# Weight parts of the expert layer made three pieces ahead, with ACT and DVE in program order

## The chip, the core and the metric

The kernel runs on one core of one Trainium2 chip. The core has a matrix engine (TensorE, called PE in the profile, with its weight loads as PEld), a vector engine (DVE), a scalar engine (ACT), a general-purpose engine (POOL), a queue engine (SP) that here only starts DMAs, and 16 DMA engines. The metric is the device time of one execution in microseconds (us); lower is better.

## The reference, cut to what matters

A trunk of two layers over 256 tokens of width 1024. Each layer has a mixer (attention and a delta rule) with a normalization, then a channel mixer with another. The channel mixer of the first layer is dense; that of the second sends each token to 2 of 8 experts. The change is in this expert layer alone:

```python
def swiglu(x, w_gate, w_up, w_down):
    return (jax.nn.silu(x @ w_gate) * (x @ w_up)) @ w_down
...
    gates = jax.nn.softmax(top_val, axis=-1)
...
        xb = xf[tok_b]
        return swiglu(xb, w_gate[e_b], w_up[e_b], w_down[e_b])
```

An expert has a gate and an up matrix of 1024 x 3584 and a down matrix of 3584 x 1024, all float32. Each expert's rows are weighted by its gate value and added to the tokens that chose it.

## The kernel before

**Pieces.** All expert weights stream once from HBM. A piece is what one DMA brings: 128 rows of 1792 columns of gate or up (896 KB), or two rows per partition of down (1 MB). `load` (line 148) takes one of eight raw buffers (seven in `ring`, one in `ring2`) and starts the DMA on SP; loads keep their program order. `halves` (line 163) makes of each half of a piece a high part `wh`, a rounded copy by ACT (line 178), and a low part `wl`, the difference by DVE (line 181). These take eight slots (four in `wpool`, four in `wpool2`), so four pieces can stand made. A float32 product is then three matmuls, high by high, high by low and low by high.

**Order of the work.** `experts` (line 981) runs over eight jobs, expert 0 first and the others in the order `TURN`. Three experts with few tokens are narrow (64 rows); the five others are wide (128 rows). Narrow and wide ones alternate: the third job follows the second as wide after narrow, and so on to the last two, both wide. The hidden width comes in two chunks of 1792. A chunk runs eight gate pieces, then three down pieces of the chunk before (the pending chunk), then eight up pieces and the four remaining down pieces. A wide piece is 12 matmuls (six per half). A narrow one is eight, since high and low tokens stand side by side; its eighth gate and up piece is not split but multiplied as float32 from the raw buffer, after `leads` (line 1115) has copied half of the four banks into `room`, and four matmuls with `shift` add those halves back.

**Side steps.** After the gate, ACT writes Silu into `hh` (line 1193); after the up, DVE multiplies it (line 1216). `to_features` (line 1126) then transposes `hh` on PE, and ACT and DVE split it into `hT`. `combine` (line 1089) splits the result `ys` of the expert before, multiplies it with a 0/1 matrix `DT` and adds it into `x_tok` on DVE (line 1100); `transposed` (line 1034) makes `DT`, DVE then PE then DVE. `dispatch` (line 1004) gathers the tokens of coming experts. These run as `side` steps, one after each gate or up piece.

**Who sets the order.** The framework's scheduler orders each engine's queue by its own estimate of when operands are ready, the program order as priority. `pin` (line 97) keeps an instruction in program order among the pinned ones of its engine. Before the change the DMAs, Silu, the `room` copies, the multiplication with Silu and a few steps of `dispatch` are pinned; the making of the parts, `hT`, `ys`, `DT` and the additions into `x_tok` are not, nor are the matmuls. The code that makes parts stands just ahead of its products:

```python
                for sub in in_pieces(wg, c, len(first or ()), narrow):
                    if narrow and sub[0] == KD - 1:
                        subs = next(downs, None)
                        moves = leads(banks)
                    products(banks, xg, narrow, *sub, x32)
                    if side and sub[0]:
                        side.pop(0)()
```

## Time and profile before

| what | value |
|---|---|
| median of 3 runs | 1490.4 us (1489.93 to 1492.49) |
| the profiled execution | 1489.22 us |
| its span, first to last instruction | 1487.1 us |
| mean granted clock of TensorE, of full speed | 0.989 |
| expert weights read by DMA | 128 gate and 128 up loads of 896 KB, 110 down loads of 1 MB and five smaller ones |

The profiled execution lies 1.2 us below the median of the runs, and 2.1 us lie outside its span. Line numbers are those of the kernel before. An engine's busy time is the union of its instructions; a wait is idle time of an engine, put down to what ended it. The buffers `ps_mm` and `ps_gd` hold gate and up sums, `ps_b` the down sums, `ps_a` transposes and other short uses.

### The profile page before, as it was taken

The numbers are of one execution on the slowest core, as the hardware profiler recorded it, in microseconds if no ns is written. First come the engines' busy times: TensorE is split into PE (matmuls) and PEld (weight loads), VectorE is DVE, ScalarE is ACT, GpSimd is POOL, SyncE is SP. The second block draws the span as 40 slices with busy tenths as digits, with TensorE's granted clock in tenths as the row PEclk, the third lists the DMA queues.
The fourth block names the chain that finished last, engine by engine and source line by source line (L and its number), as shares of the span: only waits on it lengthen the run. The fifth ranks groups of instructions, "written<-read, shape, count | busy, mean of one in ns | idle before, by whom it ended". The sixth has DMA issues, their size and how long they took to land.

```text
span 1487.1 us, 24022 instructions
## 1 busy us (share of the span) xinstructions
PE 1444.9 (97%) x8864; PEld 1230.1 (83%) x8864; DVE 1218.2 (82%) x1609; ACT 1037.7 (70%) x1553; POOL 23.8 (2%) x37
## 2 busy tenths in 40 slices
PE   8999999999999999999999999999999999999995
PEld 8978899998978898876698877688877589888884
DVE  6886655556797898989899989899989899989886
ACT  5747444456667577786797886886887878778763
POOL 1100000000000000000000000000000000000000
PEclk9999999999999999999999999999999999999998
DMA  9633455545533199999999999999999999999890
GB/s 323 220 115 121 161 194 179 196 125 189 199 108 129 50 337 346 376 359 353 416 404 375 381 359 391 377 409 404 355 370 401 349 404 415 344 350 392 291 374 33
DMA packets 89125, 433.93 MB, mean 292 GB/s; under 512 B 7817, under 2 KB 9993, under 8 KB 74913
## 3 DMA queue, kind: packets, MB, share of 16 engines
q1 hardware_dynamic: 87808, 428.54, 76.8%
q0 software_dynamic: 1184, 3.71, 0.9%
q8 instruction: 73, 1.20, 0.3%
q14 instruction: 60, 0.48, 0.1%
HBM read 431.17 MB, written 1.05 MB: 291 GB/s over the span
## 4 chain that ended last, share of the span: by engine, by line
PE 87%; DVE 7%; issue 2%; ACT 2%; DMA 0%; DVEq 0%; SPq 0%; ACTq 0%
PE ps_b L101 26%; PE ps_mm L101 25%; PE ps_gd L101 24%; PE ps_a L101 9%; DVE wl L181 4%; PE ps_a L1138 2%; ACT wh L178 1%; DVE x_in L1100 1%; PE ps_mm L567 0%; ACT junk L416 0%; DVE hT L1141 0%; ACT xT L241 0%; PE ps_gd L409 0%; PE ps_mm L671 0%; DVE o L1280 0%
## 5 line engine op out<-in xcount | busy, mean ns | idle before, releaser
L181 DVE TENSOR_TENSOR wl<-raw,wh 128x896 fp32r<-128x896 f32 (+2 forms) x851 | 927.5, 1143 | 146.7 <-ACT wh L178 139.6
L178 ACT ACTIVATE wh<-raw 128x896 fp32r<-128x896 f32 (+2 forms) x851 | 793.0, 996 | 147.4 <-PE ps_gd L101 70.9
L101 PE MATMUL ps_b<-wh,hT 128*128 128x512 f32 x816 | 232.5, 396 | 0.7 <-ACT hT L1140 0.7
L101 PE MATMUL ps_gd<-wh,xg 128*128 128x448 f32 x808 | 218.6, 368 | 0.0
L101 PE MATMUL ps_mm<-wh,xg 128*128 128x448 f32 x808 | 212.4, 372 | 0.3
L101 PEld LDWEIGHTS ps_b<-wh,hT 128*128 128x128 f32 x816 | 151.9, 188 | 39.4 <-issue 6.4
L101 PEld LDWEIGHTS ps_gd<-wh,xg 128*128 128x128 f32 x808 | 151.8, 188 | 12.9
L101 PEld LDWEIGHTS ps_mm<-wh,xg 128*128 128x128 f32 x808 | 147.6, 189 | 16.5 <-ACT wh L178 2.0
L101 PE MATMUL ps_b<-wl,hT 128*128 128x512 f32 x492 | 159.0, 399 | 2.3 <-DVE wl L181 2.2
L101 PE MATMUL ps_gd<-wl,xg 128*128 128x448 f32 x488 | 143.1, 374 | 8.9 <-DVE wl L181 7.2
L101 PE MATMUL ps_mm<-wl,xg 128*128 128x448 f32 x488 | 140.8, 369 | 0.1
L101 PEld LDWEIGHTS ps_b<-wl,hT 128*128 128x128 f32 x492 | 90.8, 188 | 32.0 <-DVE wl L181 6.7
L101 PEld LDWEIGHTS ps_gd<-wl,xg 128*128 128x128 f32 x488 | 89.0, 188 | 27.9 <-DVE wl L181 20.0
L101 PEld LDWEIGHTS ps_mm<-wl,xg 128*128 128x128 f32 x488 | 90.8, 188 | 11.7 <-DVE wl L181 4.3
L1140 ACT ACTIVATE hT<-ps_a 128x512 fp32r<-128x512 f32 (+2 forms) x52 | 27.4, 544 | 65.8 <-PE ps_a L1138 38.7
L101 PE MATMUL ps_mm<-xT,wh 128*128 128x256 f32 x448 | 70.9, 280 | 0.0
L101 PEld LDWEIGHTS ps_mm<-xT,wh 128*128 128x128 f32 x448 | 60.8, 189 | 0.4
L1141 DVE TENSOR_TENSOR hT<-ps_a,hT 128x512 fp32r<-128x512 f32 (+2 forms) x52 | 31.9, 621 | 26.7 <-ACT hT L1140 26.7
L101 PE MATMUL ps_gd<-xT,wh 128*128 128x256 f32 x320 | 50.5, 280 | 0.0
L1093 ACT ACTIVATE ys<-ps_b 128x512 fp32r<-128x512 f32 x14 | 8.4, 599 | 55.5 <-PE ps_b L101 41.3
L101 PE MATMUL ps_mm<-xT,wl 128*128 128x256 f32 x224 | 44.7, 280 | 0.0
L101 PEld LDWEIGHTS ps_gd<-xT,wh 128*128 128x128 f32 x320 | 43.1, 189 | 0.0
(407 smaller groups left out, 1654.3 us busy)
## 6 DMA issues: line engine op xcount, KB each, us to landing
raw<-in_moe_w_gate_dram SPq DMA_DIRECT2D x128, 896.0 KB, 8.7
raw<-in_moe_w_up_dram SPq DMA_DIRECT2D x128, 896.0 KB, 6.4
raw<-in_moe_w_down_dram SPq DMA_DIRECT2D x110, 1024.0 KB, 8.1
raw<-in_w_in_dram SPq DMA_DIRECT2D x24, 1024.0 KB, 6.9
raw<-in_ffn_w_gate_dram SPq DMA_DIRECT2D x11, 1024.0 KB, 5.1
raw<-in_ffn_w_up_dram SPq DMA_DIRECT2D x11, 1024.0 KB, 5.1
raw<-in_ffn_w_down_dram SPq DMA_DIRECT2D x11, 1024.0 KB, 4.9
raw<-in_w_out_dram SPq DMA_DIRECT2D x8, 1024.0 KB, 4.9
```

Source lines behind the costliest of these rows:

```text
L101: return PE.matmul(o, lhsT, rhs, start=start, stop=stop, skip_group_check=True)
L178: high = S.activation(wh[:, c:c + n], w, AF.Copy)
L181: low = V.tensor_tensor(wl[:, c:c + n], w, wh[:, c:c + n].bitcast(F32), op=ALU.subtract)
L1093: S.activation(yh, py[i], AF.Copy)
L1100: V.scalar_tensor_tensor(o, pt, jobs[n][2][:, b], o, op0=ALU.mult, op1=ALU.add)
L1138: PE.transpose(pt[:, f * w:(f + 1) * w], hv[:, f0 + f], ident[rows, rows])
L1140: S.activation(hT[:, f0:f0 + n_, 0], pv, AF.Copy)
L1141: V.tensor_tensor(hT[:, f0:f0 + n_, 1], pv, hT[:, f0:f0 + n_, 0].bitcast(F32), op=ALU.subtract)
```

## The change

A generator `stream` lists all pieces in the order in which the products use them. `made` loads one and makes its parts; `take` keeps a queue so that, when a piece is handed to its products, the three after it have been emitted. The instructions on ACT and DVE in the expert layer (making of parts, gathered tokens, `DT`, `ys`, `hT`, additions) are pinned. Silu now stands after one down piece and not two, the multiplication after one and not two, and the routing's `rest` runs as a side step in expert 0's first gate. The matmuls stay unpinned, and the order of the loads is the same.

```diff
@@ -38,6 +39,7 @@
...
+AHEAD = 3
...
@@ -176,9 +178,13 @@
             for c in range(0, m, n):
                 w = raw[:, i * m + c:i * m + c + n]
                 high = S.activation(wh[:, c:c + n], w, AF.Copy)
+                if extra:
+                    pin(high)
                 if fence_high[0] is not None:
                     order(high, fence_high[0])
                 low = V.tensor_tensor(wl[:, c:c + n], w, wh[:, c:c + n].bitcast(F32), op=ALU.subtract)
+                if extra:
+                    pin(low)
                 if fence[0] is not None:
                     order(low, fence[0])
             yield i * (nk // count), wh, wl
@@ -985,6 +991,7 @@
 
...
-                        S.activation(xg[:, k], i, AF.Copy)
+                        pin(S.activation(xg[:, k], i, AF.Copy))
...
-            V.tensor_tensor(x_, xg[:, KD - 1, 0].bitcast(F32), xg[:, KD - 1, 1].bitcast(F32), op=ALU.add)
+            pin(V.tensor_tensor(x_, xg[:, KD - 1, 0].bitcast(F32), xg[:, KD - 1, 1].bitcast(F32), op=ALU.add))
...
         def transposed(n):
             Dt = mp.tile([P, NB, P], F32R, tag="ys", name=nm("D"))
-            slots(Dt, jobs[n], True)
+            pin(slots(Dt, jobs[n], True))
             DT = mp.tile([P, NB, P], F32R, tag=f"DT{n % 2}", name=nm("DT"), bufs=1)
             pt = bank("a")
             for b in range(NB):
                 PE.transpose(pt[:, b * P:(b + 1) * P], Dt[:, b].bitcast(F32), ident)
-            V.tensor_copy(DT.rearrange("p b t -> p (b t)"), pt[:, 0:NB * P])
+            pin(V.tensor_copy(DT.rearrange("p b t -> p (b t)"), pt[:, 0:NB * P]))
             return DT
-        def in_pieces(w, c, k0=0, narrow=False):
...
-        def down_pieces(n, c, first=0, parts=1, cut=1):
...
+        def stream():
+            behind = []
+            for n in range(NE):
+                for c in range(NC):
+                    yield from ((n, 0, c, k) for k in range(KD))
+                    yield from behind[:3]
+                    yield from ((n, 1, c, k) for k in range(KD))
+                    yield from behind[3:]
+                    behind = [(n, 2, c, f) for f in range(0, NF, 2)]
+            yield from behind
+        def made(n, i, c, k):
+            cs = slice(c * CHUNK, (c + 1) * CHUNK)
+            if i == 2:
+                src = weights(n, 2)[cs].rearrange("(p j) d -> p j d", j=NF)[:, k:k + 2, :]
+                end = (n, c) == (NE - 1, NC - 1)
+                cut = 2 if end and k == NF - 2 else 1
+                return [(k + j, wh, wl) for j, wh, wl in piece(src, 2, D, 2 if end and k >= NF - TAIL else 1, cut)]
+            if first and (n, i, c) == (0, 0, 0) and k < len(first):
+                return list(first[k])
+            src = weights(n, i).rearrange("(k p) c -> p k c", p=P)[:, k:k + 1, cs]
+            if jobs[n][3] and k == KD - 1:
+                return load(src, 1, CHUNK)[0]
+            return list(piece(src, 1, CHUNK))
+        specs = stream()
+        ready = collections.deque()
+        ahead = AHEAD if extra else 1
+        def take():
+            for spec in itertools.islice(specs, ahead + 1 - len(ready)):
+                ready.append(made(*spec))
+            return ready.popleft()
...
-                S.activation(yh, py[i], AF.Copy)
-                V.tensor_tensor(yl, py[i], yh.bitcast(F32), op=ALU.subtract)
+                pin(S.activation(yh, py[i], AF.Copy))
+                pin(V.tensor_tensor(yl, py[i], yh.bitcast(F32), op=ALU.subtract))
...
-                    V.scalar_tensor_tensor(o, pt, jobs[n][2][:, b], o, op0=ALU.mult, op1=ALU.add)
+                    pin(V.scalar_tensor_tensor(o, pt, jobs[n][2][:, b], o, op0=ALU.mult, op1=ALU.add))
...
-                S.activation(hT[:, f0:f0 + n_, 0], pv, AF.Copy)
-                V.tensor_tensor(hT[:, f0:f0 + n_, 1], pv, hT[:, f0:f0 + n_, 0].bitcast(F32), op=ALU.subtract)
+                pin(S.activation(hT[:, f0:f0 + n_, 0], pv, AF.Copy))
+                pin(V.tensor_tensor(hT[:, f0:f0 + n_, 1], pv, hT[:, f0:f0 + n_, 0].bitcast(F32), op=ALU.subtract))
...
-        most = rest() if rest else None
+        most = []
+        if rest:
+            side = [lambda: None] * 2 + [lambda: most.append(rest())]
         for n, job in enumerate(jobs):
             narrow = job[3]
             rows = slice(0, 64) if narrow else slice(0, P)
             xg = xgs.pop(n)
             x32 = as_one(xg) if narrow else None
-            wg, wu = (weights(n, i).rearrange("(k p) c -> p k c", p=P) for i in range(2))
             for c in range(NC):
+                def project(banks, start):
+                    moves = ()
+                    for k in range(KD):
+                        parts = take()
+                        if narrow and k == KD - 1:
+                            moves = leads(banks)
+                        products(banks, xg, narrow, k, parts, x32)
+                        if side and k >= start:
+                            side.pop(0)()
+                    while side:
+                        side.pop(0)()
+                    return moves
+                def more(times=1):
+                    for _ in range(times if pend else 0):
+                        down(take(), *pend)
                 banks = gu_banks()
-                for k, f in enumerate(first or ()):
-                    products(banks, xg, narrow, k, f)
-                downs = down_pieces(pend[0], pend[1]) if pend else iter(())
-                subs, moves = None, ()
-                for sub in in_pieces(wg, c, len(first or ()), narrow):
-                    if narrow and sub[0] == KD - 1:
-                        subs = next(downs, None)
-                        moves = leads(banks)
-                    products(banks, xg, narrow, *sub, x32)
-                    if side and sub[0]:
-                        side.pop(0)()
-                first = None
+                moves = project(banks, 1)
                 fence[0] = fence_high[0] = None
-                while side:
-                    side.pop(0)()
                 hh = mp.tile([P, CHUNK], F32, tag="hh", name=nm("hh"))
                 if pend and not pend[3]:
                     pend[3].extend([bank("b"), bank("b")])
-
-                def more(subs=None):
-                    subs = subs or next(downs, None)
-                    if subs:
-                        down(subs, *pend)
-
-                more(subs)
+                more()
                 for move in moves:
                     move()
-                more()
                 for i, p in enumerate(banks):
                     pin(S.activation(hh[rows, i * BANK:(i + 1) * BANK], p[rows, :], AF.Silu))
-                more()
+                more(2)
                 banks = gu_banks()
                 if c == NC - 1 and groups and n + 1 not in xgs:
                     group = groups.pop(0)
                     tiles, side = dispatch([jobs[g] for g in group])
                     xgs.update(zip(group, tiles))
-                subs, moves = None, ()
-                for sub in in_pieces(wu, c, 0, narrow):
-                    if narrow and sub[0] == KD - 1:
-                        subs = next(downs, None)
-                        moves = leads(banks)
-                    products(banks, xg, narrow, *sub, x32)
-                    if side:
-                        side.pop(0)()
-                while side:
-                    side.pop(0)()
-                more(subs)
+                moves = project(banks, 0)
+                more()
                 for move in moves:
                     move()
-                more()
                 for i, p in enumerate(banks):
                     h = hh[rows, i * BANK:(i + 1) * BANK]
                     pin(V.tensor_tensor(h, h, p[rows, :], op=ALU.mult))
-                for subs in downs:
-                    down(subs, *pend)
+                more(3)
                 hT, side = to_features(hh, narrow)
                 if pend and pend[1] == NC - 1:
                     side += combine(pend[0], pend[3], DT)
@@ -1230,10 +1252,8 @@
         while side:
             side.pop(0)()
         f0 = c * NF
-        TAIL = 4
-        for subs in itertools.islice(down_pieces(n, c), (NF - TAIL) // 2):
-            down(subs, *pend)
-        subs = [(f0 + f, wh, wl) for subs in down_pieces(n, c, NF - TAIL, 2, 2) for f, wh, wl in subs]
+        more((NF - TAIL) // 2)
+        subs = [(f0 + f, wh, wl) for _ in range(TAIL // 2) for f, wh, wl in take()]
         extra.clear()
 
         par = ring.tile([P, 2, D], F32, tag="raw", name=nm("par"))
...
-        return most
+        return most[0] if most else None
```

## Rows read from the trace of the kernel before

**Rows 1.** the page: its span, and busy time, share and instructions of each engine

```profile
span 1487.1 us, 24022 instructions
PE 1444.9 (97%) x8864; PEld 1230.1 (83%) x8864; DVE 1218.2 (82%) x1609; ACT 1037.7 (70%) x1553; POOL 23.8 (2%) x37
```

**Rows 2.** busy time by stretch: length, PE, PEld, DVE, ACT, POOL (instructions), clock, DMA share, GB/s

```profile
617.50:848.00 230.50, 227.03 (x1047) 184.60 (x1047) 210.51 (x225) 182.25 (x242) 0.00 (x0) 1.00 0.97 381
...
1312.20:1434.40 122.20, 121.50 (x585) 107.03 (x584) 110.21 (x118) 94.39 (x113) 0.00 (x0) 1.00 0.93 347
```

**Rows 3.** busy time by stretch, same columns: one pair of experts in five stretches

```profile
848.00:905.50 57.50, 57.24 (x253) 44.22 (x252) 51.11 (x55) 49.08 (x64) 0.00 (x0) 1.00 0.98 373
905.50:938.80 33.30, 31.27 (x135) 22.33 (x134) 28.18 (x31) 20.78 (x30) 0.00 (x0) 1.00 0.96 368
938.80:963.80 25.00, 24.14 (x95) 15.89 (x94) 23.25 (x25) 23.58 (x29) 0.00 (x0) 1.00 0.98 381
963.80:1017.10 53.30, 53.30 (x257) 46.90 (x256) 50.48 (x52) 43.71 (x53) 0.00 (x0) 1.00 1.01 412
1017.10:1079.30 62.20, 61.66 (x313) 54.73 (x312) 58.11 (x65) 46.10 (x70) 0.00 (x0) 1.00 0.97 372
```

**Rows 4.** busy time by stretch of the down sums alone: length, PE, PEld, DVE, ACT

```profile
848.00:905.50 57.50, 24.90 (x103) 18.78 (x102) 0.00 (x0) 0.00 (x0) 1.00 0.98 373
905.50:938.80 33.30, 10.40 (x43) 7.50 (x42) 1.37 (x2) 1.20 (x2) 1.00 0.96 368
938.80:963.80 25.00, 7.05 (x27) 4.62 (x26) 0.00 (x0) 0.00 (x0) 1.00 0.98 381
963.80:1017.10 53.30, 12.59 (x51) 9.10 (x50) 0.00 (x0) 0.00 (x0) 1.00 1.01 412
1017.10:1079.30 62.20, 15.65 (x65) 11.54 (x64) 1.37 (x2) 1.20 (x2) 1.00 0.97 372
```

**Rows 5.** timeline of PE: start, length of the merged run, instruction, count

```profile
585.81 1.10 PE L101 MATMUL ps_b<-wh,hT 128*128 128x512 f32 x4
...
587.21 1.09 PE L101 MATMUL ps_b<-wh,hT 128*128 128x512 f32 x4
...
594.15 0.98 PE L101 MATMUL ps_mm<-wh,xg 128*128 128x448 f32 x4
...
595.38 0.98 PE L101 MATMUL ps_gd<-wh,xg 128*128 128x448 f32 x4
...
596.61 0.59 PE L101 MATMUL ps_a<-D,xs 128*128 128x192 f32 x4
597.03 0.39 PE L101 MATMUL ps_mm<-wh,xg 128*128 128x448 f32 x1
```

**Rows 6.** busy time of raw-buffer instructions alone, same columns; PE is the unsplit part

```profile
905.50:938.80 33.30, 3.22 (x8) 1.01 (x8) 22.73 (x21) 15.25 (x18) 0.00 (x0) 1.00 0.96 368
```

**Rows 7.** waits, 905.5 to 938.8 us: total us, times, longest

```profile
ACT ys L1093 <- PE ps_b L101: 4.8, 1, 4.8
...
ACT hh L1193 <- PE ps_mm L101: 2.1, 1, 2.1
...
ACT room L1122 <- PE ps_mm L101: 2.0, 1, 2.0
```

**Rows 8.** timeline of DVE around the second narrow gate's Silu

```profile
932.98 3.50 DVE L181 TENSOR_TENSOR wl<-raw,wh 128x1024 fp32r<-128x1024 f32 x3 [0.38 <-ACT wh L178]
939.73 4.23 DVE L181 TENSOR_TENSOR wl<-raw,wh 128x1024 fp32r<-128x1024 f32 x4 [3.26 <-ACT wh L178]
```

**Rows 9.** timeline of ACT, the same stretch

```profile
931.88 2.95 ACT L178 ACTIVATE wh<-raw 128x1024 fp32r<-128x1024 f32 x3
936.92 0.97 ACT L1193 ACTIVATE hh<-ps_mm 64x448 f32<-64x448 f32 x2 [2.09 <-PE ps_mm L101]
938.64 5.26 ACT L178 ACTIVATE wh<-raw 128x1024 fp32r<-128x1024 f32 x6
```

**Rows 10.** waits, 1017.1 to 1079.3 us, with a combining step: total, times, longest

```profile
DVE x_in L1100 <- PE ps_a L101: 0.9, 2, 0.7
```

More of the change, by code (lines that the diff above doesn't have):

```diff
@@ L1 @@
+import collections
 import itertools
@@ L987, in experts @@
         NC = FE // CHUNK
+        TAIL = 4
         def xg_tile(narrow):
@@ L1040, in transposed @@
                 PE.transpose(pt[:, b * P:(b + 1) * P], Dt[:, b].bitcast(F32), ident)
-            V.tensor_copy(DT.rearrange("p b t -> p (b t)"), pt[:, 0:NB * P])
+            pin(V.tensor_copy(DT.rearrange("p b t -> p (b t)"), pt[:, 0:NB * P]))
             return DT
-        def in_pieces(w, c, k0=0, narrow=False):
-            for k in range(k0, KD):
-                src = w[:, k:k + 1, c * CHUNK:(c + 1) * CHUNK]
-                yield k, load(src, 1, CHUNK)[0] if narrow and k == KD - 1 else piece(src, 1, CHUNK)
         def products(outs, xg, narrow, k, parts, x32=None):
@@ L1066, in products @@
                         mm(o[j], x_, w[:, j * BANK:(j + 1) * BANK], k == 0 and w is wh, False)
-        def down_pieces(n, c, first=0, parts=1, cut=1):
-            wd = weights(n, 2)[c * CHUNK:(c + 1) * CHUNK].rearrange("(p j) d -> p j d", j=NF)
-            for f in range(first, NF, 2):
-                yield [(f + j, wh, wl) for j, wh, wl in piece(wd[:, f:f + 2, :], 2, D, parts, cut if f == NF - 2 else 1)]
+        def stream():
[28 more added lines that the diff above has]
+            return ready.popleft()
         def down(subs, n, c, hT, py):
```

## The prediction

> **What bounds the kernel now.** I read the page first, then busy time by stretch, then the down sums alone, then the timelines and waits where an engine pauses. On the page PE is busy for 97% of the span, its weight loads for 83% and DVE for 82% [rows 1]; so PE looks full. The stretches say more. The steady part of the expert layer repeats: a narrow and a wide expert take 230.5 and 231.3 us in the first two of three pairs, and the last wide expert 122.2 us [rows 2, 3]. I cut one pair into the narrow expert's first chunk, its second gate, its second up, and the wide expert's two chunks [rows 3].
>
> Next, what PE needs in each. In undisturbed work six matmuls of 512 columns start 1.40 us after one another (585.81 to 587.21), six of 448 columns 1.23 us; that is 0.233 and 0.205 us each. Four gathering matmuls of 192 columns take 0.42 us, 0.105 each; transposes are taken at the same, an estimate [rows 5]. The unsplit narrow part takes 3.2 us a phase [rows 6], its four shift matmuls 0.8 at 0.205. The code gives the gate and up matmuls (56 a narrow phase, 96 a wide one), the trace the down ones: 103, 43, 27, 51 and 65 [rows 4]; a combining step adds eight of 512 columns. So:
> first narrow chunk: 112 x 0.205 + 103 x 0.233 + 8.0 + 14 transposes 1.5 = 56.5 of 57.5 us;
> second narrow gate: 11.5 + 51 x 0.233 + 4.0 + 1.7 = 29.1 of 33.3;
> second narrow up: 11.5 + 27 x 0.233 + 4.0 = 21.8 of 25.0;
> wide chunks: 39.4 + 51 x 0.233 + 1.5 = 52.8 of 53.3, and 39.4 + 73 x 0.233 + 1.7 + 32 x 0.105 = 61.5 of 62.2.
> PE needs 221.7 of 231.3 us. It is the bound everywhere except in the narrow expert's second chunk, where DVE has 28.2 and 23.3 us of work [rows 3], and where PE loses 7.4 of its 9.6 us.
>
> PE's busy share hides this: it is 24.1 of 25.0 us in the second up for 21.8 us of matmuls. The Trainium skill ("Perfetto Trace Analysis", Identifying the Most-Contended Engine) says that matmul busy time is a poor measure of headroom and that load time is better; the loads there are busy 15.9 of 25.0 us, so the trace agrees. By busy time alone the pair would hold 231.3 - 227.6 = 3.7 us, 11 us for three pairs.
>
> **Why DVE pauses there.** In the second narrow gate DVE ends three subtractions at 936.5 us and starts the next at 939.73, after 3.26 us of waiting for ACT [rows 8]. ACT had made those three halves, then stood 2.09 us before Silu, which waits for PE's unsplit part and shifts, and worked on Silu until 938.64 [rows 9]. So only three halves lay between the `room` copies and Silu; DVE ran dry and PE with it. The same stretch has ACT standing 4.8 us before `ys` and 2.0 before `room`, with weight copies behind it [rows 7].
>
> **The change, part by part.**
> *Three pieces ahead.* Four pieces fit the eight slots before and after, so no depth is added: the copy of piece n+3 waits for the matmuls of piece n-1. What changes is which copies stand ahead of a waiting instruction. When ACT comes to `room`, the three down pieces are already copied; the first up piece is copied before Silu. DVE then has eight halves, at 3.50 / 3 = 1.17 us each [rows 8] 9.4 us. ACT is through Silu, counted from the last split gate product, after half the `room` copies 1.0, the unsplit part 3.2, one narrow down piece 8 x 0.233 = 1.9, shifts 0.8 and Silu 938.64 - 936.92 = 1.7 [rows 6, 9], 8.6 us, plus a copy of about 1.0 (2.95 / 3). So 9.6 against 9.4: DVE pauses about 0.2 us, not 3.6 (3.26 and 0.38 [rows 8]).
> *Pinned side steps.* These are new waits. The subtraction for `ys` now stands behind the part three pieces ahead, and the addition into `x_tok` right behind it, waiting for a PE product; likewise the two DVE steps of `DT` with transposes between them. Until PE answers, every later subtraction queues behind. The nearest row for that answer is 0.9 us for two waits, 0.7 the longer [rows 10]: I take 0.45 each, three per expert, 1.35 us; the ends are 0 (PE does it meanwhile) and 0.7 each, 2.1. `hT` copies wait for transposes behind one gate piece while three pieces stand made (3 x 8 x 0.205 = 4.9 us of narrow PE work): nothing, unless PE has caught up with DVE, and then DVE still holds three pieces. Gathered tokens and the unsplit part's sum: the same cover.
> *Earlier Silu and multiplication.* Names only: banks come free a down piece (1.9 to 2.8 us) sooner, while PE has made pieces to work on.
> *Loads.* SP issues the same DMAs in the same order; each waits for the raw buffer of the eighth load before it. A faster DVE frees them sooner. A pair moves, by length times rate of its five stretches, 88.3 MB [rows 3]; at the 412 GB/s of the first wide chunk that is 214 us, below PE's 221.7, so the loads still fit. The register that picks an expert is read on SP just before that expert's first load, as before.
> *Routing's rest in the first gate, and first parts pinned behind the gathering steps.* Both only move short work at the start of the layer. I take 0, between -2 and +2, a subtraction or two (1.17 each [rows 8]) either way.
>
> **The sum.** Second narrow gate: DVE's 28.2 plus 1.35 of new waits, 0.2 at Silu and 0.4 left over, about 30.2 of 33.3: 3.1 us gained. Second up: 23.3 plus 0.3, 1.4 gained. In the first narrow chunk and the wide chunks PE's floor leaves 1.0 + 0.5 + 0.7 = 2.2; I take less than half, 1.0, since the new waits fall there too. A pair gains 5.5 us, three 16.5, and the last wide expert 0.5 (its matmuls need 384 x 0.205 + 168 x 0.233 + transposes 2.9 = 120.7 of 122.2). From the profiled execution's 1489.2 us that leaves 1472.2; its runs' median lies 1.2 higher, so **1473 us**.
>
> **Rivals.**
> *All of it.* If every stretch reaches its floor (PE's, DVE's 23.3 in the up), a pair gains 231.3 - (56.5 + 29.1 + 23.3 + 52.8 + 61.5) = 8.1; if made pieces carry DVE's excess over, 9.6. Three pairs and about 1.5 at the last expert: 26 to 30 us, 1462 us. For it: the pauses are all of one kind. Against: the new waits are certain, only their price isn't.
> *Nothing moves.* The copies may only exchange places with the waits, or DMA may be the bound: its share is 0.96 to 1.01 in every stretch [rows 3]. Then 1490 us. Against the second: in the stretch of 0.96 it moved 368 GB/s, in that of 1.01 412, so the share does not tell the rate. The Trainium skill ("DMA: Bandwidth & Descriptors", Bandwidth) lets the HBM side bind at about 358 GB/s. By that rule a pair's bytes would take 246 us and there would be no gain; the measured 231.3 us and 412 GB/s contradict it, and the measurement decides.
> *Slower: PE stops at the side steps of the wide experts.* The matmuls are not pinned. If the scheduler leaves the products with `ys` and the transposes of `DT` in program order, PE, which is the bound there, waits until DVE has made the part three pieces ahead and then the side step. That is three places in each of the last four wide experts and one in expert 0, 13 in all. Each costs at most a wide piece, 12 x 0.205 = 2.46 us: 32 us, less the 17 gained, 1505 us. It decides above 17 / 13 = 1.3 us a place. For it: ACT can copy that part only once PE frees its slots. Against: slots come free by halves, and the scheduler, which knows DVE's new order, can put other products first.
>
> **How the numbers follow.** The forecast gets 0.58 (1465 to 1481), all of it 0.14, nothing 0.12, slower 0.16. The measurement tells about 0.2%, 3 us, from no change. So faster 0.72, same 0.12, slower 0.16. The range reaches from 1456, which is 1490.4 less 30, less 2 at the start and less 2 for what the rounding of the spacings leaves, to 1492, just past no change, and leaves out most of the slower case.
>
> **What would show it.** Right: pairs of about 226 us; the second narrow gate near 30 us and its up below 24; DVE's pause before the first subtraction after Silu below 1 us; `ys` on ACT waiting little; wide chunks within 1 us of 53.3 and 62.2. Wrong: PE waiting for DVE at `ys` or `DT` inside wide gates; pauses of DVE before the additions above 1 us; or narrow stretches as long as before with raw buffers empty, DMA then being the bound.

## The result, and the profile after

The changed kernel takes 1507.56 us (median of four runs, 1504.16 to 1511.51) against 1490.52 before: a ratio of 1.0098, 95% interval 1.0077 to 1.012. It is 1% slower; 1473 us had been forecast, within 1456 to 1492.

The page of the changed kernel, its span and busy times, answers to [rows 1]; its profiled execution is the slowest of the four (1511.51 us):

```profile
span 1509.4 us, 24147 instructions
PE 1459.8 (97%) x8864; PEld 1240.6 (82%) x8864; DVE 1220.9 (81%) x1609; ACT 1047.5 (69%) x1553; POOL 23.8 (2%) x37
```

No engine has more instructions of its own (the total also counts waiting and issuing ones), and the shares are nearly the same. So I cut both spans at the same places: the first routing product, the first gate product, then the first gate product of each narrow expert and of the last wide one. Busy time by stretch (length, PE, PEld, DVE, ACT, POOL, clock, DMA share, GB/s), the kernel before:

```profile
504.90:522.80 17.90, 16.39 (x91) 14.87 (x91) 16.12 (x56) 12.38 (x20) 0.00 (x0) 0.73 0.12 37
522.80:628.40 105.60, 105.58 (x517) 94.76 (x517) 93.99 (x111) 81.39 (x107) 0.00 (x0) 0.98 0.96 354
628.40:858.40 230.00, 226.53 (x1046) 184.19 (x1044) 210.34 (x223) 183.19 (x241) 0.00 (x0) 1.00 0.98 381
858.40:1089.60 231.20, 227.51 (x1045) 184.02 (x1044) 211.02 (x224) 183.16 (x241) 0.00 (x0) 1.00 0.98 382
1089.60:1320.20 230.60, 226.89 (x1046) 184.06 (x1045) 208.46 (x220) 181.38 (x232) 0.00 (x0) 1.00 0.97 380
1320.20:1487.10 166.90, 150.46 (x703) 127.80 (x701) 135.28 (x150) 107.20 (x132) 0.00 (x0) 0.97 0.74 280
```

The same six stretches of the changed kernel; the pairs answer to [rows 2]:

```profile
509.60:529.70 20.10, 18.79 (x91) 16.28 (x91) 14.75 (x65) 6.88 (x14) 0.00 (x0) 0.63 0.00 1
529.70:636.30 106.60, 106.58 (x517) 95.37 (x518) 94.47 (x99) 87.19 (x114) 0.00 (x0) 0.97 0.94 350
636.30:871.70 235.40, 230.22 (x1045) 186.57 (x1044) 210.81 (x224) 184.90 (x241) 0.00 (x0) 0.98 0.93 375
871.70:1107.70 236.00, 230.85 (x1045) 186.61 (x1044) 211.11 (x224) 185.59 (x241) 0.00 (x0) 0.98 0.94 374
1107.70:1341.60 233.90, 227.17 (x1046) 183.94 (x1045) 210.80 (x224) 184.41 (x233) 0.00 (x0) 1.00 0.94 378
1341.60:1509.40 167.80, 150.71 (x703) 128.07 (x701) 135.63 (x148) 109.74 (x132) 0.00 (x0) 0.97 0.72 273
```

The spans differ by 22.3 us. Of these 4.7 lie before the first routing product (504.9 against 509.6), in instructions that both kernels have in the same order; the last section comes back to them. The routing stretch adds 2.2, the first wide expert 1.0, the three pairs 5.4, 4.8 and 3.3, the rest 0.9: 17.6 us in the expert layer.

Of the pairs' 13.5 us, the narrow experts' second gates account for 13.4; elsewhere gains and losses cancel (the second ups are 0.8 to 2.4 us shorter, the narrow experts' first ups 1.5 longer, each wide expert 0.9 to 1.0 longer). A second gate here runs from its first gate product to its first up product; the prediction's stretch of 33.3 us began 6.3 us earlier, with down pieces. It takes 29.0 us in each pair before; the third one before, and then all three after, with the same columns:

```profile
1143.00:1172.00 29.00, 26.97 (x116) 18.82 (x115) 23.00 (x26) 21.32 (x30) 0.00 (x0) 1.00 0.87 328
```

```profile
690.30:724.80 34.50, 30.89 (x117) 21.88 (x116) 25.28 (x29) 19.27 (x28) 0.00 (x0) 0.85 0.57 229
925.80:960.30 34.50, 30.89 (x118) 21.88 (x117) 25.24 (x29) 19.36 (x28) 0.00 (x0) 0.85 0.94 371
1161.80:1193.20 31.40, 27.40 (x118) 19.33 (x117) 25.27 (x29) 19.28 (x28) 0.00 (x0) 1.00 0.63 253
```

Read the clock column first. The third gate runs at full clock and is 2.4 us longer than before: that is the order of the work. The other two do the same work at a mean clock of 0.85 and lose 3.1 more each. Together 5.5 + 5.5 + 2.4 = 13.4 us.

The third gate on DVE (start, length, instruction, and in brackets the idle time before it and what ended it) shows the order; line numbers are now those of the kernel that ran:

```profile
1173.41 0.68 DVE L1127 TENSOR_TENSOR ys<-ps_b,ys 128x512 fp32r<-128x512 f32 x1
1176.39 1.41 DVE L1133 SCALAR_TENSOR_TENSOR x_in<-ps_a,sorted,x_in 128x512 f32<-128x512 f32 x2 [2.31 <-PE ps_a L103]
1177.71 0.68 DVE L1127 TENSOR_TENSOR ys<-ps_b,ys 128x512 fp32r<-128x512 f32 x1
1178.98 1.41 DVE L1133 SCALAR_TENSOR_TENSOR x_in<-ps_a,sorted,x_in 128x512 f32<-128x512 f32 x2 [0.59 <-PE ps_a L103]
1180.31 2.35 DVE L185 TENSOR_TENSOR wl<-raw,wh 128x1024 fp32r<-128x1024 f32 x2
1182.58 0.42 DVE L1007 TENSOR_TENSOR D<-io,sorted 128x256 fp32r<-128x256 f32 x1
1183.70 0.42 DVE L1048 CAST DT<-ps_a 128x256 fp32r<-128x256 f32 x1 [0.70 <-PE ps_a L1047]
1184.04 6.63 DVE L185 TENSOR_TENSOR wl<-raw,wh 128x1024 fp32r<-128x1024 f32 x6
1193.87 2.09 DVE L185 TENSOR_TENSOR wl<-raw,wh 128x896 fp32r<-128x896 f32 x2 [3.20 <-ACT wh L180]
```

And on PE:

```profile
1174.89 0.62 PE L103 MATMUL ps_a<-ys,DT 128*128 128x512 f32 x2
...
1175.96 0.63 PE L103 MATMUL ps_a<-ys,DT 128*128 128x512 f32 x2
1177.29 1.89 PE L103 MATMUL ps_a<-ys,DT 128*128 128x512 f32 x4 [0.70 <-ACT ys L1126]
...
1181.58 0.73 PE L103 MATMUL ps_b<-wl,hT 128*128 128x512 f32 x2 [1.94 <-DVE wl L185]
...
1185.31 0.74 PE L103 MATMUL ps_b<-wl,hT 128*128 128x512 f32 x2 [1.18 <-DVE wl L185]
```

DVE, three pieces ahead, has `ys` ready at 1174.1 and comes to the addition. PE is still at older gate products and reaches those of `ys` at 1174.89 and 1175.96. Nothing may pass the pinned addition, so DVE stands (waits idle) 2.31 us, then 0.59, then 0.70 before `DT`: 3.6 us, and 4.9 in the two gates at the lower clock. In the same gate of the kernel before, DVE ran halves of weights between these steps and did not wait:

```profile
1152.52 1.40 DVE L1100 SCALAR_TENSOR_TENSOR x_in<-ps_a,sorted,x_in 128x512 f32<-128x512 f32 x2
1153.84 1.08 DVE L181 TENSOR_TENSOR wl<-raw,wh 128x896 fp32r<-128x896 f32 x1
1154.84 0.68 DVE L1094 TENSOR_TENSOR ys<-ps_b,ys 128x512 fp32r<-128x512 f32 x1
1155.44 1.08 DVE L181 TENSOR_TENSOR wl<-raw,wh 128x896 fp32r<-128x896 f32 x1
1156.44 1.40 DVE L1100 SCALAR_TENSOR_TENSOR x_in<-ps_a,sorted,x_in 128x512 f32<-128x512 f32 x2
```

In the changed kernel the halves of the down pieces (1180.31) are then late, and PE stands 1.94 and 1.18 us for them: the lead has become a wait on the other side. The pause before the first subtraction after Silu [rows 8] is still there, 3.20 us.

### The profile page after: what moved, and what is told of

Its sections match the earlier page's. It is cut to its first block, busy times and chain, and to the rows that moved or that the text cites. A ratio compares the mean times of both kernels' runs of the same rounds, so it can differ in the third digit from the quotient of the medians.

```text
span 1509.4 us, 24147 instructions
## 1 busy us (share of the span) xinstructions
PE 1459.8 (97%) x8864; PEld 1240.6 (82%) x8864; DVE 1220.9 (81%) x1609; ACT 1047.5 (69%) x1553; POOL 23.8 (2%) x37
## 4 chain that ended last, share of the span: by engine, by line
PE 87%; DVE 6%; ACT 2%; issue 2%; DMA 1%; SPq 0%; DVEq 0%; ACTq 0%
PE ps_mm L103 26%; PE ps_gd L103 25%; PE ps_b L103 24%; PE ps_a L103 9%; DVE wl L185 4%; PE ps_a L1171 2%; ACT wh L180 1%; DMA raw<-in_moe_w_down_dram 1%; DVE x_in L1133 1%; PE ps_mm L573 0%; ACT junk L422 0%; DMA x_in<-in_x_dram 0%; PE ps_gd L415 0%; PE ps_mm L677 0%; ACT xT L247 0%
## 5 line engine op out<-in xcount | busy, mean ns | idle before, releaser
L180 ACT ACTIVATE wh<-raw 128x896 fp32r<-128x896 f32 (+2 forms) x851 | 803.6, 996 | 186.5 <-PE ps_gd L103 73.3
L103 PE MATMUL ps_b<-wh,hT 128*128 128x512 f32 x816 | 239.0, 400 | 0.5 <-ACT wh L180 0.3
L103 PE MATMUL ps_gd<-wh,xg 128*128 128x448 f32 x808 | 212.9, 368 | 0.0
L103 PE MATMUL ps_b<-wl,hT 128*128 128x512 f32 x492 | 165.7, 410 | 10.5 <-DVE wl L185 10.1
L103 PEld LDWEIGHTS ps_gd<-wl,xg 128*128 128x128 f32 x488 | 89.9, 189 | 20.8 <-DVE wl L185 13.5
L1174 DVE TENSOR_TENSOR hT<-ps_a,hT 128x512 fp32r<-128x512 f32 (+2 forms) x52 | 31.7, 619 | 12.7 <-ACT hT L1173 12.7
L1031 ACT ACTIVATE xg<-ps_a 128x256 fp32r<-128x256 f32 (+1 forms) x60 | 18.2, 353 | 30.7 <-PE ps_a L103 30.6
```

Source lines behind the costliest of these rows:

```text
L103: return PE.matmul(o, lhsT, rhs, start=start, stop=stop, skip_group_check=True)
L180: high = S.activation(wh[:, c:c + n], w, AF.Copy)
L1031: pin(S.activation(xg[:, k], i, AF.Copy))
L1174: pin(V.tensor_tensor(hT[:, f0:f0 + n_, 1], pv, hT[:, f0:f0 + n_, 0].bitcast(F32), op=ALU.subtract))
```

## The experiments

Each ratio is against the kernel before, run beside it on the same chip. Gates are the three narrow second gates, from one profiled execution of each run.

**Which pins?** Four runs take pins away. In the first, the steps of `combine` and `DT` are free:

```diff
-                pin(S.activation(yh, py[i], AF.Copy))
+                S.activation(yh, py[i], AF.Copy)
...
-                    pin(V.scalar_tensor_tensor(o, pt, jobs[n][2][:, b], o, op0=ALU.mult, op1=ALU.add))
+                    V.scalar_tensor_tensor(o, pt, jobs[n][2][:, b], o, op0=ALU.mult, op1=ALU.add)
```

(likewise the subtraction for `ys`, D and DT).

> The changed kernel with the combining step and DT (ys copy and subtraction, additions into x_tok, both DVE steps of DT) no longer pinned; everything else as changed. Theory A (the loss is made in the narrow experts' second gate, where the pinned ys copy holds ACT 5.0 us and the pinned additions hold DVE 2.9 us in front of the down parts, and PE then idles and loses its clock): the three second gates, 34.5, 34.5 and 31.4 us from first gate product to first up product, fall to 30 or less with a granted clock of 1.00, and the time to 1488 to 1497 us. Theory B (the pinned weight parts cost by themselves, spread over all stretches): 1503 us or more, second gates at most 2 us shorter.

It took 1504.27 us, ratio 1.0079 (1.0058 to 1.0099). The gates fell to 29.3, 29.3 and 29.6 us, as A says; the time is B's, and its interval overlaps that of the changed kernel. In the profile the expert layer was still 11.1 us longer than before, 4.3 of it from the last wide expert to the end; the pairs' wide second gates, which hold the same steps, take 33.1 to 33.2 us (32.2 to 32.3 before). So these pins make the narrow gates long, and with them gone part of the loss lies elsewhere.

In the second, all new pins go (halves, gathered tokens, `hT`, `combine`, `DT`) and the queue stays.

> The changed kernel without any of its new pins: the queue three pieces ahead, the earlier Silu and multiplication and the later routing rest stay, the scheduler orders ACT and DVE freely as before. Theory A: the queue alone costs nothing, 1485 to 1495 us. Theory C (the new program order, Silu one down piece earlier and parts emitted ahead, costs by itself): 1500 us or more.

It took 1493.62 us, ratio 1.0007 (0.9996 to 1.0019). The queue alone neither gains nor costs; what loses is the fixed order on top of it. Its second gates are longer too (30.8 to 31.2 us at clocks of 0.94 to 0.95), but the ups behind them are shorter by 0.3 to 3.1.

In the third, only the halves are free again (its edit is shown); in the fourth only the halves are pinned:

```diff
-                if extra:
-                    pin(high)
...
-                if extra:
-                    pin(low)
```

> The changed kernel with only the halves of weights free (ACT's copy and DVE's subtraction); the side steps stay in program order and the queue stays. Theory A (a pinned side step hurts because it stands behind pinned halves made three pieces ahead): with the halves free the narrow second gates fall to 29 to 31 us (34.5 in the changed kernel, 29.0 before), the start is back near 523, time 1489 to 1496. Theory B (the side steps' fixed order among themselves is enough to hold TensorE up): the gates stay above 32, time 1499 or more.

> The changed kernel with all side steps free (ys, additions, D, DT, hT, gathered tokens) and only the halves of weights in program order. Theory A (the loss of the gates needs the side steps pinned as well; that of the start needs only the halves): narrow second gates at 30 us or less, start between 523 and 529, time 1490 to 1504, the more the start is late. Theory B (halves in fixed order are by themselves what holds TensorE up): gates above 32, time 1502 or more.

With the side steps pinned it took 1494.3 us, ratio 1.0009 (0.9992 to 1.0027); with the halves pinned 1498.47 us, 1.0058 (1.0037 to 1.0079), gates 30.8 to 31.2. Either group alone costs less than both (1.0098, though the halves' interval touches it), and the side steps alone cost nothing that can be told; that a free half can go past a step that waits would explain it. A fits the first of the two but for the start (528.3 us, not 523) and gates a little longer than it said (30.8 to 31.6); in the second the gates lie between A and B.

**The queue under the pins.** All pins, nothing made ahead (`ahead = 0`):

> The changed kernel with the queue at no piece ahead: each piece's parts are emitted right before its own products, all pins kept. If the pieces ahead are what makes pinning bearable, every side step of a gate now holds ACT or DVE with no part made beyond it: 1530 us or more. If ACT and DVE run ahead anyway, as the slots allow, 1500 to 1515 us, near the changed kernel.

It took 1607.31 us, ratio 1.077 (1.074 to 1.0799), as the first of the two theories has it. The queue carries the pinned order; two and one ahead are below.

**The start.** The halves made before the first gate has ended are free:

```diff
-                if extra:
+                if extra and fence_high[0] is None:
                     pin(high)
```

> The changed kernel in which the halves of weights made before the first gate has ended are free again; everything after that keeps its program order. Theory A (the start loses because the first pieces' halves stand behind the gathering steps, so the ring of raw buffers stays full and the loads of the next pieces begin 14 us later): the first gate product is back at 523 us (changed kernel 529.7, before 522.8), the loads begin near 519 us again, and the time falls by 5 to 7 us to 1500 to 1503; the narrow second gates stay at 34. Theory B (the later start is a lower clock of the stretch before it, not the order): the first gate product stays at 528 or later, time 1505 to 1510.

It took 1505.64 us, ratio 1.009 (1.0059 to 1.0122). A falls. ACT copied the first halves at 515.60 again, but the first gate product came at 527.7, because the first routing product already stood at 508.8. From the one to the other it is 18.9 us here (clock 0.67), 17.9 before (0.73) and 20.1 after (0.63). The first halves' pins cost about nothing. The run brought something else; its second gates are those of the changed kernel:

```profile
688.00:719.30 31.30, 27.32 (x117) 19.27 (x116) 25.22 (x29) 19.18 (x28) 0.00 (x0) 1.00 0.62 248
920.40:951.70 31.30, 27.29 (x117) 19.28 (x116) 25.24 (x29) 19.28 (x28) 0.00 (x0) 1.00 1.00 398
1153.20:1186.70 33.50, 29.88 (x117) 21.08 (x117) 25.30 (x29) 19.28 (x28) 0.00 (x0) 0.90 0.59 236
```

Again 31.3 us at full clock, and more only where the clock fell, now in the third gate.

**The buffer of `ys`.** In the changed kernel ACT's second `ys` copy waits 4.98 us for PE to free the only buffer. A second one:

```diff
-                ys = mp.tile([P, 2, 512], F32R, tag="ys", name=nm("ys"))
+                ys = mp.tile([P, 2, 512], F32R, tag=f"ys{i}" if i else "ys", name=nm("ys"), bufs=1)
```

> The changed kernel, all pins kept, but the second part of the combining step gets a ys buffer of its own (two small routing tiles share other buffers to make room). Theory A, with the single ys buffer as the link: ACT's wait of 5.0 us before the second ys copy falls below 1.5 us, the down parts are copied that much earlier, the second gates fall to 31 us or less, the time to 1493 to 1501 us. If instead the additions on DVE are the link, the second gates stay above 33 us and the time stays at 1504 to 1510 us.

It took 1503.21 us, ratio 1.0069 (1.0046 to 1.0092), gates 32.5 to 33.5 at clocks of 0.90 to 0.95: between the two theories, and its interval overlaps that of the changed kernel. ACT's wait went, but in the third gate DVE stood 2.34 and 0.59 us before the additions and 1.86 before `DT`. The buffer alone was not the cause.

**The place of the steps.** With two `ys` buffers and all pins, the side steps are cut: `ys` is made with the first two side steps, D one step before its transposes (part of the edit):

```diff
+                    cuts, adds = combine(pend[0], pend[3], DT)
+                    for i in range(2):
+                        side[i] = lambda s=side[i], c=cuts[i]: (c(), s())
+                    side += adds
```

> The changed kernel with a second ys buffer (as in the run with two of them, 1503.2 us, gates 32.5 to 33.5), and with the pinned steps of combine cut in two: ys is copied and subtracted with the first two side steps, its products and the additions follow in their places, and D is written one side step before its transposes. All pins stay. Theory A (TensorE reaches products whose operand DVE has not made, because that step stands behind three pieces' halves in DVE's order): the waits of TensorE for ys and D go, the narrow second gates fall to 30 to 32 us, time 1497 to 1501, with the start still late. Theory B (the additions, which make DVE wait for TensorE, are what costs, and they stay): gates stay at 32.5 or more, time 1502 or more.

It took 1486.02 us, ratio 0.9969 (0.995 to 0.9987): faster than both kernels, and more than A asked. The gates:

```profile
684.20:712.80 28.60, 27.06 (x118) 19.35 (x118) 25.18 (x29) 18.98 (x28) 0.00 (x0) 1.00 0.68 269
913.20:941.80 28.60, 27.05 (x118) 19.33 (x117) 25.21 (x29) 19.40 (x28) 0.00 (x0) 1.00 1.01 418
1141.90:1170.50 28.60, 27.06 (x118) 19.34 (x117) 25.18 (x29) 18.97 (x28) 0.00 (x0) 1.00 0.68 271
```

and the additions of the third one on DVE:

```profile
1154.70 0.74 DVE L1142 SCALAR_TENSOR_TENSOR x_in<-ps_a,sorted,x_in 128x512 f32<-128x512 f32 x1
1155.95 0.75 DVE L1142 SCALAR_TENSOR_TENSOR x_in<-ps_a,sorted,x_in 128x512 f32<-128x512 f32 x1 [0.51 <-PE ps_a L103]
...
1157.22 1.41 DVE L1142 SCALAR_TENSOR_TENSOR x_in<-ps_a,sorted,x_in 128x512 f32<-128x512 f32 x2 [0.19 <-PE ps_a L103]
```

The stands are down from 3.6 to 0.7 us and the gate is 2.8 us shorter. Against the changed kernel the second gates of the three pairs fall by 14.7 us in the narrow experts and by 2.6 in the wide ones, and no other gate or up, summed likewise, changes by more than 0.8: the edit acts where the cut steps are. Does the order do it without the second buffer (`ys` made one step ahead), and does the split gain without queue and pins?

> The changed kernel with its single ys buffer and all pins, and only the order of the side steps moved: the first ys is made with the first side step, the second ys right behind the first products, D right behind the second products, each one side step ahead of TensorE's use of it. Theory A (what costs is the distance in program order between a step that vector and scalar make and the products that use it): most of the gain of the split run (1486.0) comes without the second buffer, narrow second gates 28.5 to 30, time 1486 to 1493. Theory B (the single buffer is what ACT's second copy waits for, 4.98 us in the changed kernel, and the order alone does not help): gates 32 or more, time 1499 or more.

> The kernel before, without queue and without new pins, with the second ys buffer and the split side steps. Theory A (the gain of the split run over the kernel before needs the queue and the pins; the kernel before already places its free steps where they fit): within 2 us of the kernel before, 1490 to 1493, narrow second gates near 29. Theory B (the split alone is what gains, and queue and pins add nothing): 1484 to 1488, pairs of 229 to 230 us.

With one buffer it took 1493.57 us, ratio 1.0006 (0.9989 to 1.0023), gates 29.1 to 29.6; the gates are A's, the time lies 0.6 us beyond its range. The order takes back the loss; the gain came only with the buffer as well, in the run above, whose second `ys` and D also stand earlier than here. The kernel before with the split took 1490.24 us, 0.9982 (0.997 to 0.9995): a small gain, at the edge of what A says. Its 0.18% cannot be told from the 0.31% of the split run; the 0.56% of a run below, with two ahead, is clear of it.

**How many ahead?** `AHEAD` at 2 with the split, at 2 and at 1 without:

> The split run (second ys buffer, all pins) with two pieces ahead in place of three. Theory A (a piece made ahead is what lets DVE work while ACT waits for Silu): with two the pause of DVE before its first subtraction after Silu comes back (0 in the split run, 3.3 before), second gates 29 to 31, time 1489 to 1500. Theory B (depth does not matter once the side steps stand early): time within 2 us of the split run, 1484 to 1488.

> The changed kernel, all pins, side steps where they were, with two pieces ahead in place of three. Theory A (a pinned side step costs because it stands behind the halves of the pieces made ahead of it; the fewer there are, the sooner vector and scalar come to it): narrow second gates 28.5 to 30.5 us against 31.4 at full clock with three, time 1490 to 1499. Theory B (the pins themselves cost, whatever the depth): gates at 31 or more, time 1500 or more.

> The changed kernel with one piece ahead. Theory A has two effects against each other here: side steps stand behind one piece only, but TensorE has only one piece to work on while DVE waits for it at a pinned step; with none ahead (1607) the second effect costs 100 us, with two ahead it is nil. I expect it to win: gates 31 or more and losses in the wide gates too, 1500 to 1540. Theory B (only the distance counts): 1488 to 1497.

With the split and two it took 1486.83 us, ratio 0.9944 (0.9925 to 0.9964), the best ratio of all, though its interval overlaps that of three; B holds there, and the premise of A was wrong, since the split run does pause after Silu (3.65 us). Without the split it took 1511.69 us, 1.0102 (1.0085 to 1.0119), with two, and 1529.3 us, 1.0221 (1.0201 to 1.024), with one. A of the second falls: its gates stayed at 32.5 to 34.0 us (clocks 0.95 and 0.85) and wide stretches grew too. With one ahead, two gates at full clock take 31.7 us against 31.4 with three. So the distance in made pieces does not by itself set the gates.

**The additions alone.** First freed, then moved one side step later and still pinned:

```diff
-                    pin(V.scalar_tensor_tensor(o, pt, jobs[n][2][:, b], o, op0=ALU.mult, op1=ALU.add))
+                    late.append(lambda o=o, pt=pt, b=b: pin(V.scalar_tensor_tensor(o, pt, jobs[n][2][:, b], o, op0=ALU.mult, op1=ALU.add)))
```

> The changed kernel with three ahead, with the additions into x_in alone free; ys, D and DT stay pinned. Theory A (the late ys and D are what TensorE waits for): narrow second gates stay above 30.5 us, time 1500 to 1508. Theory B (DVE standing before the additions, 2.29 and 0.59 us in the second narrow gate, is what puts everything behind it back): gates at 30 or less, time 1490 to 1498.

> The changed kernel (three ahead, one ys buffer, all pins), with the additions into x_in alone moved one side step later, still pinned: the first pair behind the next gate piece's halves, the second pair just ahead of the transposes of D. Theory B (vector, which is ahead of TensorE and is the bound in this gate, stands 2.3 and 0.6 us before the additions until TensorE comes to the products, and that time is lost): vector's stands before the additions fall below 1 us, the narrow second gates to 29 to 30 us, time 1492 to 1499. Theory A (the late ys and D are what costs): gates at 31 or more, time 1503 or more.

> The split run with two pieces ahead (1486.8 us, 0.9944 of the kernel before in its call), with the additions one side step later as well. Theory B: the stands that are left there (0.5 us) go too, second narrow gates 28 or less, 1483 to 1486. Theory A: no more to gain, within 2 us of 1486.8 against the same kernel before (a ratio of 0.993 to 0.996).

Freed, it took 1507.92 us, ratio 1.0085 (1.0069 to 1.0102). PE, DVE and ACT kept exactly the order of the changed kernel, so the run does not tell A from B; it is a second measurement of the changed order, with gates of 33.4, 31.4 and 31.4 us at clocks of 0.90, 1.00 and 1.00. Moved, it took 1500.48 us, 1.0048 (1.0029 to 1.0068). The move did half of what B asked: no halves come between the first products and their additions there (the piece three ahead is the unsplit one), so DVE stood 2.31 us as before; the 0.59 went and `DT`'s wait fell to 0.53:

```profile
697.73 1.41 DVE L1137 SCALAR_TENSOR_TENSOR x_in<-ps_a,route,x_in 128x512 f32<-128x512 f32 x2 [2.31 <-PE ps_a L103]
...
701.92 1.40 DVE L1137 SCALAR_TENSOR_TENSOR x_in<-ps_a,route,x_in 128x512 f32<-128x512 f32 x2
...
704.18 0.42 DVE L1048 CAST DT<-ps_a 128x256 fp32r<-128x256 f32 x1 [0.53 <-PE ps_a L1047]
```

The gate of these rows takes 30.5 us at full clock; the other two 31.9 and 31.8 at 0.95. With the split and two ahead the later additions gain no more: it took 1490.59 us, 0.9977 (0.9961 to 0.9992), and the wide second gates are 33.3 us in place of 32.1.

**What the gates have in common.** These are the runs with all pins and three pieces ahead. DVE has 25.1 to 25.3 us of work in each of their gates. In a gate at full clock, its stands before additions and `DT`, and the gate's length:

| run | DVE stands | gate |
|---|---|---|
| changed | 3.6 | 31.4 |
| additions late | 2.8 | 30.5 |
| split, one buffer | 1.2 | 29.1 |
| split | 0.7 | 28.6 |

The length follows the stands nearly one for one: 2.9 us less standing, 2.8 us less gate. The split also makes `ys` and D earlier, so the late operands are a rival. PE's own waits weigh the two: from the changed third gate to that of the split run its waits for `wl` fall from 3.1 to 1.1 us, its wait for `ys` from 0.7 to nothing. So the late operand can be about a quarter of it. The rule does not hold where steps are free: with only the halves pinned a gate at full clock takes 30.8 us with 0.6 of stands, since PE there waits 1.6 us for D and DVE 2.2 for `wh`.

## Why the prediction was wrong

*What bounds the kernel.* Right on the place: in the narrow expert's second gate PE waits for DVE's `wl` (1.9 us before, 3.1 in the changed third gate), and PE is the bound in the wide chunks: in the changed kernel's wide second gates of the pairs DVE stands about 2.5 us before additions and `DT` and PE idles only 0.2. Too large was the room. I took 221.7 us of PE work a pair from the spacing of undisturbed matmuls, so 9.6 to gain, over the 3.7 that PE's busy time leaves. No run came near it: in the split run the second pair saves 2.6, with PE busy for 225.7 of 228.6 us.

```profile
859.20:1087.80 228.60, 225.73 (x1045) 183.92 (x1044) 210.76 (x224) 185.83 (x241) 0.00 (x0) 1.00 0.97 386
```

For that choice I had leaned on the Trainium skill ("Perfetto Trace Analysis", Identifying the Most-Contended Engine), by which matmul busy time is a poor measure of headroom; here it was the closer of the two.

*Three pieces ahead.* This step failed too, but the queue alone made no loss (1.0007). The pause of 3.26 us was to fall to 0.2; it is 3.20 in the changed kernel's third gate and 3.65 in the second one of the split run, whose up is nevertheless 2.1 us shorter than before (26.4 against 28.5). DVE pauses there because it is ahead: in the changed third gate PE works without a gap from 1185.3 us to the end of the gate. So the pause was not the loss that the forecast took it for: in the split run, which still has it, the second gate and up together are 2.6 us shorter than before, of 4.5 forecast. The 1.4 us at the second up came, as 2.3 in the changed kernel's second pair; the wide expert behind it then took 1.0 more.

*Pinned side steps.* **This step turned the sign.** I priced them at 0.45 us a wait, 1.35 an expert, with ends of 0 and 2.1. In the third narrow expert DVE stands 3.6 us, beyond the upper end, and the gate is 2.4 us longer where 3.1 less was forecast. With all pins kept, moving these steps takes the ratio from 1.0098 to 1.0006, and to 0.9969 with the second buffer. The lower clock of the other two gates, 3.1 us each in this execution, stood in no term of the forecast. The row behind the price [rows 10] came from an order in which the scheduler had kept additions and products apart; it bounds no order that puts them back to back. I had named the sign ("pauses of DVE before the additions above 1 us") and not asked what it would cost the engine that was just then the bound.

*hT, loads.* `hT` was rightly taken at nothing: DVE stands for it neither in the narrow second gates nor in the pairs' wide first gates. DMA did not become the bound: its share fell to 0.57 and 0.63 in the first and third of the long gates, and where DVE ran ahead it carried 418 GB/s, above the 358 GB/s that the forecast took from the Trainium skill ("DMA: Bandwidth & Descriptors", Bandwidth). That section gives this figure as the share of a core with both cores of an HBM domain streaming; this kernel runs on one core.

*Start.* Taken at 0 between -2 and +2. The stretch took 2.2 us more, at a clock of 0.63 in place of 0.73. The run with freed additions has the same order and took 18.5 us at 0.73, against 17.9 before: some 0.6 us belong to the order, and the rest went with the lower clock of that execution.

*Rivals.* "PE stops at the side steps of the wide experts" gave 1505 us for a measured 1507.6, from the wrong place: the wide second gates grew by 0.1 to 0.5 us. What stops is DVE, and it costs time at the narrow ones. That the number lies close is luck. "Nothing moves" is what the queue does alone.

Not settled: why halves in fixed order cost 0.6 to 0.8% when the side steps of `combine` are free, though the split run has the same halves pinned and gains; and the wide stretches with fewer pieces ahead.

## What to carry to other kernels

An engine that runs ahead of another loses its lead at a step in a fixed order that needs an answer from the one behind. Make the operand early, take the answer late, with independent work between; a deeper queue did not do this here: with the steps in their old places, three pieces ahead lost as much as two. A pause of an engine that is ahead is no loss to recover: look at whether its consumer has work in that time. And a wait measured under one order does not bound the wait under another.

## What was not expected of the hardware

TensorE's granted clock differs between gates with the same instructions in the same order. In the changed kernel it was 0.85, 0.85 and 1.00, with the first halves free 1.00, 1.00 and 0.90, with 3.1, 3.1 and 2.2 us between 34.5, 33.5 and the 31.3 to 31.4 at full clock. The means mix its two levels, 2.4 and 1.2 GHz: in the second gate two products of 512 columns right behind PE's wait of 1.94 us take 1.22 us, in the third (1181.58 above), behind the same wait, 0.73.

```profile
945.55 1.22 PE L103 MATMUL ps_b<-wl,hT 128*128 128x512 f32 x2 [1.94 <-DVE wl L185]
```

So the wait alone does not decide; what does is open. The split run's three gates stayed at full clock in its profiled execution.

Before the expert layer, where nothing is changed, the first routing product starts at 504.90 us before and at 509.57 after. That it isn't the change is seen from two runs, the queue alone and the late additions with all pins:

```profile
504.37 1.95 PE L103 MATMUL ps_mm<-rw,xTf 128*128 128x8 f32 x16 [0.25 <-ACT xTf L847]
```

```profile
504.84 1.95 PE L103 MATMUL ps_mm<-rw,xTf 128*128 128x8 f32 x16 [0.25 <-ACT xTf L851]
```

So 4.7 of the 22.3 us between the two profiles belong to the execution, not to the change. Over these experiments the kernel before spread from 1487.7 to 1497.4 us; a difference of some 5 us is read from medians and intervals, not from two profiles.
